# adaLN products of layer 1: from the attention stage to beside the first MLP, in pieces of 256 columns of all four quarters

## The chip, the cores and the metric

The kernel runs on one core of a Trainium2 chip. The metric is the device time of one execution in microseconds (us), lower is better. The program names five engines: PE (TensorE, matrix products), DVE (VectorE), ACT (ScalarE), POOL (GpSimd) and SP (SyncE, which issues the DMA transfers). Each engine runs its own instructions strictly in the order in which they stand; semaphores make one wait for another.

## The reference, cut to what matters

Two layers over 1280 tokens (1024 latent, 256 context) of 1024 channels. Each layer is a mixer and a squared-ReLU MLP, each with a normalised and modulated input and a gated output. The modulation (adaLN) of layer l is

```python
mod = jax.nn.silu(cond) @ ada_w[l] + ada_b[l]      # (1024) @ (1024, 6144), for c and for c_ctx
shift1, scale1, gate1, shift2, scale2, gate2 = split(mod, 6)
h  = rms_norm(x, g1) * (1 + scale1) + shift1
x  = x + gate1 * mixer(h)                          # layer 0: DeltaNet and window attention; layer 1: RG-LRU
h2 = rms_norm(x, g2) * (1 + scale2) + shift2
x  = x + gate2 * (square(relu(h2 @ ff_w1)) @ ff_w2)
```

`cond` has two rows: `c` for the latent tokens, `c_ctx` for the context tokens. `ada_w[l]` is 24 MB. The products of layer 1 are not needed before the end of layer 0's MLP, where layer 1's first norm is applied.

## The kernel before, in words

All is float32 by name. The large products split each factor into a high and a low part of type fp32r and add three products (`gemm_tile`, L463): high by high (L466), low by high (L467) and high by low (L468). Weights come by SP in halves of 256 KB into `wraw` buffers; ACT casts the high part `whi`, POOL or DVE subtracts to get `wlo` (`wload`, L439).

The stages are: input projection of layer 0 (to about 460 us of the span), the attention stage `dn_attention` (460 to 936 us), the output projection (`OutProj`, `hhi`/`hlo` are its input's two parts, made by `split`, L564 and L565), the first MLP (`ff`), the RG-LRU mixer `mix1`, its output projection and the second MLP.

The attention stage goes over five groups of DeltaNet tiles in the order `DN_ORDER`. A group has two halves, called half-steps here. In each half-step `dn_post` prepares two tiles (L1588, L1596, L1604), `dn_step` advances the states (L1635, L1642, L1645; the new state is added on DVE at L1647), and `att_next` lets the window attention go on by one piece (L1791, L1828, L1832; softmax on ACT and DVE, L1818 on POOL or DVE). `finish` and `finish2` complete a tile: a chain of small DVE and POOL operations, transposes on PE (L1681) and a product into `x` at L1684.

Between them `ada_next` advances the adaLN products. `ada` handles a third `q` of the 6144 columns at a time, that is 2048 columns as four quarters `j` of 512. Its 16 pieces of 512 KB each are loaded by L297 into buffers that `whi`/`wlo` use later, and each piece is two products at L300: 32 columns of weights (`sc`, the silu of the conditions) against 512 columns of `adaw`, one for each of two quarters, into 32 partitions each of the PSUM bank `ps_ad`. Five thirds are done in this stage: two of layer 0 and three of layer 1, 80 pieces. At a third's end the sums are copied (L304), transposed (L307, four products) and biased (L310). The list `RATES` says how many pieces are let go after each step.

In the MLP, `ff1` makes one block of 128 hidden channels (24 products for each of three token tiles, of 512, 512 and 256 tokens) into banks `ps_mm`, and `ff2` multiplies two blocks back into 8 output chunks by 3 token tiles, six products for each into banks `ps_w` (L518 to L520), which DVE adds into `x` (L521). The last `ff2` also feeds the next norm: ACT squares each chunk (L396), PE sums it over channels (L332, into a `ps_w` bank held meanwhile), and the sums are spread again (L368, L369, one more bank) for `apply`. PSUM has four `mm` and four `w` banks here.

The order on each engine is made by a scheduler that simulates the program when it is built and takes, of what is ready by its simulation, what has the highest priority; mostly that is the order in the source.

Of the kernel before, what the change touches and what calls it, by code (L numbers as in the profile page):

```python
# [8 lines left out]
F32 = mybir.dt.float32  # L9
F32R = mybir.dt.float32r  # L10
AF = mybir.ActivationFunctionType
# [9 lines left out]
KC = 8  # L21
# [86 lines left out]
def pack(I):  # L108
    f = lambda a: np.ascontiguousarray(np.asarray(a))
    o = {}  # L110
    x = np.concatenate([f(I["x_sample"])[0], f(I["x_prompt"])[0]], axis=0)
    o["xT"] = f(x.T.reshape(KC, 128, T).transpose(1, 0, 2))

    def chunks(w, cols=None):
        w = f(w)
        K, N = w.shape
        return f(w.reshape(K // 128, 128, N // 128, 128).transpose(2, 1, 0, 3).reshape(N // 128, 128, K))

    w_in = f(I["ab_w_in"])[0]
    hp = np.arange(512).reshape(2, 2, 2, 64).transpose(0, 2, 1, 3).reshape(512)  # L120
    qa, ka, va, gate = [w_in[:, 512 * i + hp] for i in range(4)]
    ab = w_in[:, 2048:2080]
    qb = w_in[:, 2080:2592].reshape(D, 2, 4, 64).transpose(0, 2, 1, 3).reshape(D, 512)
    kb, vb = w_in[:, 2592:2720], w_in[:, 2720:2848]
    o["w_in0"] = chunks(np.concatenate([ka, qa, kb, vb, va, qb, gate], axis=1))
    o["w_ab"] = f(ab.reshape(KC, 128, 32).transpose(1, 0, 2).reshape(128, 256))
    wo = f(I["ab_w_out"])[0]
    wob = wo[512:].reshape(2, 4, 64, D).transpose(1, 0, 2, 3).reshape(512, D)
    o["w_out0"] = chunks(np.concatenate([wo[hp], wob], axis=0))
    o["w_in1"] = chunks(f(I["c_w_in"])[0])  # L130
    o["w_out1"] = chunks(f(I["c_w_out"])[0])
    o["ff1"] = np.stack([chunks(f(I["ff_w1"])[l]) for l in range(2)])
    o["ff2"] = f(f(I["ff_w2"]).reshape(2, NFC, 128, D))
    aw = f(I["ada_w"])
    o["ada"] = f(aw.reshape(2, KC, 128, 3, 2048).transpose(0, 3, 1, 2, 4).reshape(6, KC, 128, 2048)[1:])
    o["ada0"] = f(aw[0, :, :2048].reshape(KC, 128, 2, KC, 128).transpose(3, 1, 0, 2, 4).reshape(KC, 128, 2048))
    lw = np.zeros((8, 128, 2, 2, 128), np.float32)
    for gi, nm in enumerate(("lru_w_a", "lru_w_x")):
        w = f(I[nm])[0]
        for d in range(2):  # L140
            for n in range(16):
                lw[n // 2, 64 * (n % 2):64 * (n % 2) + 64, d, gi, 64 * (n % 2):64 * (n % 2) + 64] = w[d, n]
    o["lruw"] = f(lw.reshape(8, 128, 512))
    p = np.zeros((128, NPAR), np.float32)

    def put(n, v):
        a, w = PARAMS[n]
        p[:, a:a + w] = v

    cols = lambda v: f(v).reshape(-1, 128).T  # L150
    for l in range(2):
        put(f"n1g{l}", cols(f(I["norm1_g"])[l]))
        put(f"n2g{l}", cols(f(I["norm2_g"])[l]))
        put(f"adab{l}", cols(f(I["ada_b"])[l]))
    put("cond", np.stack([cols(f(I["c"])[0]), cols(f(I["c_ctx"]))], axis=-1).reshape(128, 16))
    cw, cb = f(I["ab_conv_w"])[0], f(I["ab_conv_b"])[0]
    perm = np.concatenate([512 + hp, hp, 1024 + hp])
    put("abcw", cw[:, perm].reshape(4, 12, 128).transpose(2, 1, 0).reshape(128, 48))
    put("abcb", cols(cb[perm]))
    put("dtb", f(I["dn_dt_bias"])[0].reshape(1, 16))  # L160
    put("alog", f(I["dn_a_log"])[0].reshape(1, 16))
    two = lambda v: np.concatenate([f(v)[0]] * 2)[:, None]
    put("qng", two(I["attn_q_norm_g"]))
    put("kng", two(I["attn_k_norm_g"]))
    put("dng", two(I["dn_norm_g"]))
    put("ccw", f(I["c_conv_w"])[0].reshape(4, 8, 128).transpose(2, 1, 0).reshape(128, 32))
    put("ccb", cols(f(I["c_conv_b"])[0]))
    d8 = lambda v: f(v).reshape(2, 8, 128).transpose(2, 0, 1).reshape(128, 16)
    put("lba", d8(f(I["lru_b_a"])[0]))
    put("lbx", d8(f(I["lru_b_x"])[0]))  # L170
    put("lam", d8(f(I["lru_lambda"])[0]))
    put("h0", d8(f(I["state_lru"])[0, 0]))
    put("sink", f(I["attn_sink"])[0].reshape(1, 8))
    o["par"] = p
    o["con"] = make_consts()
    o["drow"] = make_decay_rows()
    o["rope"] = np.stack(make_rope(), axis=1)
    o["amask"] = make_amask()
    ck = f(I["cache_k"])[0, 0]
    o["ckT"] = f(ck.transpose(1, 2, 0).reshape(128, 256))  # L180
    o["cv"] = f(f(I["cache_v"])[0, 0].reshape(2, 128, 128))
    sd = f(I["state_delta"])[0, 0]
    o["s0"] = f(sd.reshape(2, 4, 2, 64, 64).transpose(2, 3, 0, 1, 4).reshape(128, 512))
    return o
# [105 lines left out]
def ada(g, l, q, alloc, tag="w"):  # L290

    nc = g.nc
    ps = bank(g, tag)
    for k in range(KC):
        for jj in range(2):
            w = alloc()
            nc.sync.dma_start(w.rearrange("p j n -> p (j n)"), g.A["ada"][3 * l + q - 1, k, :, 1024 * jj:1024 * jj + 1024])  # L297
            for i in range(2):
                j = 2 * jj + i
                nc.tensor.matmul(ps[32 * j:32 * j + 32, :], g.sc[:, k, :], w[:, i, :], start=k == 0, stop=k == KC - 1,  # L300
                                 skip_group_check=True)
            yield
    row = wraw(g)
    nc.vector.tensor_copy(row, ps)  # L304
    pt = bank(g, tag)
    for s in range(4):
        nc.tensor.transpose(pt[:, 128 * s:128 * s + 128], row[:, 128 * s:128 * s + 128], g.con["ident"])  # L307
    b = g.par[f"adab{l}"][:, 16 * q:16 * q + 16].rearrange("p (j s) -> p j s", s=4)
    for c in range(2):
        nc.vector.tensor_tensor(  # L310
            g.mod[l][:, 16 * q:16 * q + 16, c].rearrange("p (j s) -> p j s", s=4),
            pt.rearrange("p (s j x) -> p j s x", s=4, j=4)[:, :, :, c], b, op=ALU.add)
    yield


def mod_cols(g, l, which):
# [160 lines left out]
            evac(o, ti, ps[:cols, :tw])  # L477


def ff(g, l, xt, hhi, hlo, Gt, pend, after):  # L480
    nc = g.nc
    pool = g.fp
    hid = {}
    w2 = {}

    def ff1(*cs):
# [3 lines left out]
        for ti, (t0, tw) in enumerate(TT):  # L490
            for c in cs:
                hh, hl = hid[c]
                ps = bank(g, "mm")
                gemm_tile(g, ps[:, :tw], *ws[c], hhi[ti], hlo[ti])
                if pend and c == cs[-1]:
                    pend.pop(0)()
                r = pool.tile([128, 512], F32, tag="ffr", name="ffr", bufs=2)
                nc.scalar.activation(r[:, :tw], ps[:, :tw], AF.Relu)  # L498
                nc.scalar.activation(hh[:, t0:t0 + tw], r[:, :tw], AF.Square)  # L499
                s = pool.tile([128, 512], F32, tag="ffs", name="ffs", bufs=2)  # L500
                nc.vector.tensor_tensor(s[:, :tw], r[:, :tw], r[:, :tw], op=ALU.mult)  # L501
                nc.gpsimd.tensor_tensor(hl[:, t0:t0 + tw], s[:, :tw], hh[:, t0:t0 + tw], op=ALU.subtract)  # L502
# [50 lines left out]
class OutProj:  # L553
# [13 lines left out]
    def finish(self, cut, Gt, after):  # L567

        g, nc, ws = self.g, self.g.nc, self.ws
        xt = []  # L570
# [21 lines left out]
                evac(o, ti, ps)  # L592

        pairs = [(o, ti) for o in range(4) for ti in range(3)]
        run(pairs[:8], KC - 1)
        for p in pairs[8:]:
            run([p])
        ws += [wload(g, self.wsrc[o]) for o in range(4, KC)]
        for ti in range(3):
# [36 lines left out]
    return after, left, h  # L636


def block(g, l, op, cut, after):

    nc = g.nc
    At, Bt, Gt = mod_cols(g, l, 2)
    step, left, h = norm_steps(g, (At, Bt), ff_scratch(g), {1: 4, 2: 4}, {1: 5, 2: 6})
    xt = op.finish(cut, g.mod[l][:, 16:24, :], step)
    ff(g, l, xt, *h["h"], Gt, left, lambda o, ti: after(o, ti, xt[ti]))


def ff_pools(g, es, order):
# [11 lines left out]
def emit(nc, tc, A, stages=None, dbg=None):  # L660
    with ExitStack() as es:
# [2 lines left out]
        g.Dx = g.dp.tile([128, KC, T], F32, name="dx")  # L664
        mix = mix0(g, A["xT"], es)
        g.hp = es.enter_context(tile_pool(g, "hp", side="right"))
        psum_cfg(g, es, mm=4, w=4)
        ab = mod_cols(g, 1, 1)[:2]

        def end1(o, ti, x):  # L670
            if o % 2:
# [2 lines left out]

        with ExitStack() as e2:
            ff_pools(g, e2, ("fp", "wx"))
            step, left, h1 = norm_steps(g, ab, ff_scratch(g), {1: 2, 2: 3}, {1: 5, 2: 7})

            def end0(o, ti, x):
                step(o, ti, x)  # L680
                if o % 4 == 3:
                    t0, tw = TT[ti]
# [3 lines left out]
            for ti in range(3):  # L686
                for k in (0, 2, 4):
                    op.split(ti, k, k + 2)
            block(g, 0, op, 6, end0)
        with ExitStack() as e2:  # L690
            op = mix1(g, h1["h"], left, e2)
        with ExitStack() as e2:
# [836 lines left out]
LATE, OPEN = 0, 0  # L1529
PS = dict(w=3, ad=1, s2=2)  # L1530
NB = dict(XW=3, QI=3, VS=3, kt=3, aP=7)
RATES = [3, 0, 0, 2, 0, 1, 0, 0, 0, 0, 0, 5, 1, 0, 0, 3, 1, 4, 3, 6, 3, 10, 8, 9, 2, 8, 1, 3, 5, 3]
PRI = dict(ada=20, att=-100, step=-1000, post=-200, post0=-200, post1=0, fin=0, late=0)


def dn_attention(g, es, open_mix):
# [198 lines left out]
        na[0] += 1  # L1735
        return g.wp.tile([128, 2, 512], F32, tag=("whi0", "wlo0", "whi1", "wlo1")[na[0] % 4], name="adaw")

    ada_left = (x for l, q in ((0, 1), (0, 2), (1, 0), (1, 1), (1, 2)) for x in ada(g, l, q, aw, "ad" if "ad" in PS else "w"))
    rates = list(RATES)
    for gr in DN_ORDER:  # L1740
        step_group(gr)
# [135 lines left out]
```

## Time and profile before

| | |
|---|---|
| median of three runs | 3308.31 us (3306.94 to 3312.88) |
| the profiled execution, its own time | 3308.6 us |
| its span in the trace | 3306.8 us |
| PE busy | 3150.0 us, 95% |
| DVE, ACT, POOL busy | 1783.5, 1117.5, 714.3 us |
| mean granted clock of PE | 0.976 of full speed |

The span is the time from the first to the last instruction in the trace; the execution's own time is 1.8 us longer. "Busy" is the time in which at least one instruction ran on the engine. Products overlap in PE's pipeline, so what a product costs in a stream is read from start to start, not from its duration.

### The profile page before, as it was taken

What the parts mean: (1) busy time and instruction counts of PE and PEld (TensorE: products, weight loads), DVE (VectorE), ACT (ScalarE), POOL (GpSimd) and SP (SyncE); (2) the same over time, 40 slices, a digit from 0 to 9 for tenths busy, and PEclk for the clock granted to TensorE, in tenths of its full rate; (3) what the DMA queues carried; (4) which work ended last, traced back from release to release, by engine and by line L of the source; (5) the groups of instructions that cost most, each with busy time, mean ns of one, the idle gap of its engine ahead of it and who ended that gap; (6) DMA issues with size and microseconds to landing.
All of it is one profiled execution on the core that took longest, in us unless ns stands there. A gap on an engine that the chain in (4) does not pass through costs nothing.

```text
span 3306.8 us, 50448 instructions
## 1 busy us (share of the span) xinstructions
PE 3150.0 (95%) x20311; PEld 2555.8 (77%) x20311; DVE 1783.5 (54%) x3080; ACT 1117.5 (34%) x2004; POOL 714.3 (22%) x637
## 2 busy tenths in 40 slices
PE   8989966899999999999999999998999999999999
PEld 5867754665568788888888877886778888888888
DVE  5549887667633544444444447778164444444444
ACT  5455523453332321212121236787142121212121
POOL 0000004455432321212121211000142222222220
PEclk9999987999999999999999999999999999999999
DMA  5356777446951011101010121111211111111111
GB/s 201 86 144 171 182 182 207 127 125 212 285 195 33 32 39 32 45 32 45 33 45 32 45 74 41 40 36 43 82 39 45 39 42 36 41 36 40 38 39 70
DMA packets 219272, 273.90 MB, mean 83 GB/s; under 512 B 71578, under 2 KB 125626, under 8 KB 219038
## 3 DMA queue, kind: packets, MB, share of 16 engines
q1 hardware_dynamic: 219038, 270.68, 27.2%
q8 instruction: 159, 2.61, 0.3%
q14 instruction: 75, 0.61, 0.1%
HBM read 223.69 MB, written 46.92 MB: 82 GB/s over the span
## 4 chain that ended last, share of the span: by engine, by line
PE 76%; DVE 8%; DMA 3%; ACT 3%; issue 2%; POOL 1%; SPq 1%; DVEq 0%; ACTq 0%; POOLq 0%
PE ps_mm L466 13%; PE ps_mm L467 13%; PE ps_mm L468 13%; PE ps_w L518 9%; PE ps_w L519 9%; PE ps_w L520 9%; DVE prod L1473 2%; PE ps_ad L300 2%; PE ps_w L1832 1%; PE ps_w L1828 1%; PE ps_w L332 1%; DVE Vinv L1474 1%; DMA adaw<-ada 1%; PE ps_w L1604 1%; PE ps_s L1791 1%
## 5 line engine op out<-in xcount | busy, mean ns | idle before, releaser
L466 PE MATMUL ps_mm<-hhi,whi 128*128 128x512 f32 (+2 forms) x2768 | 991.1, 359 | 21.0 <-ACT hhi L564 13.5
L467 PE MATMUL ps_mm<-hlo,whi 128*128 128x512 f32 (+2 forms) x2768 | 990.1, 358 | 11.0 <-POOL hlo L427 10.8
L468 PE MATMUL ps_mm<-hhi,wlo 128*128 128x512 f32 (+2 forms) x2768 | 987.8, 358 | 0.7 <-POOL wlo L457 0.7
L521 DVE SCALAR_TENSOR_TENSOR x<-ps_w,mod,x 128x512 f32<-128x512 f32 (+1 forms) x768 | 504.1, 660 | 590.9 <-PE ps_w L520 590.9
L466 PEld LDWEIGHTS ps_mm<-hhi,whi 128*128 128x128 f32 (+1 forms) x2768 | 525.8, 190 | 105.2 <-ACT hhi L564 13.9
L467 PEld LDWEIGHTS ps_mm<-hlo,whi 128*128 128x128 f32 (+1 forms) x2768 | 526.0, 190 | 92.9 <-POOL hlo L427 14.3
L468 PEld LDWEIGHTS ps_mm<-hhi,wlo 128*128 128x128 f32 (+1 forms) x2768 | 526.2, 190 | 79.8 <-issue 6.4
L519 PE MATMUL ps_w<-hidl,whi 128*128 128x512 f32 (+1 forms) x1536 | 546.5, 356 | 1.7 <-POOL hidl L502 1.7
L518 PE MATMUL ps_w<-hidh,whi 128*128 128x512 f32 (+1 forms) x1536 | 545.8, 355 | 0.0
L520 PE MATMUL ps_w<-hidh,wlo 128*128 128x512 f32 (+1 forms) x1536 | 543.8, 354 | 0.0
L502 POOL TENSOR_TENSOR hidl<-ffs,hidh 128x512 fp32r<-128x512 f32 (+1 forms) x192 | 226.5, 1180 | 1217.4 <-ACT hidh L499 977.8
L498 ACT ACTIVATE ffr<-ps_mm 128x512 f32<-128x512 f32 (+1 forms) x192 | 100.4, 523 | 902.7 <-PE ps_mm L468 883.6
L453 ACT CAST whi<-wraw 128x512 fp32r<-128x512 f32 x365 | 211.8, 617 | 516.4 <-PE ps_w L519 301.0
L501 DVE TENSOR_TENSOR ffs<-ffr 128x512 f32<-128x512 f32 (+1 forms) x192 | 164.3, 855 | 331.6 <-ACT ffr L498 327.9
L518 PEld LDWEIGHTS ps_w<-hidh,whi 128*128 128x128 f32 x1536 | 290.5, 189 | 45.7 <-issue 1.4
L519 PEld LDWEIGHTS ps_w<-hidl,whi 128*128 128x128 f32 x1536 | 290.4, 189 | 45.0 <-POOL hidl L502 2.5
L520 PEld LDWEIGHTS ps_w<-hidh,wlo 128*128 128x128 f32 x1536 | 289.7, 189 | 41.9 <-issue 0.6
L457 POOL TENSOR_TENSOR wlo<-wraw,whi 128x512 fp32r<-128x512 f32 (+1 forms) x157 | 210.4, 1361 | 259.7 <-ACT whi L453 157.7
L457 DVE TENSOR_TENSOR wlo<-wraw,whi 128x512 fp32r<-128x512 f32 x208 | 147.8, 733 | 90.9 <-ACT whi L453 90.8
L499 ACT ACTIVATE hidh<-ffr 128x512 fp32r<-128x512 f32 (+1 forms) x192 | 107.4, 560 | 5.8
L580 DVE SCALAR_TENSOR_TENSOR x<-ps_mm,mod,x 128x512 f32<-128x512 f32 (+1 forms) x40 | 25.9, 655 | 149.0 <-PE ps_mm L468 138.5
L300 PE MATMUL ps_ad<-adaw,sc 128*32 128x512 f32 x320 | 81.7, 653 | 18.8 <-DMA adaw<-ada 18.8
(377 smaller groups left out, 3272.4 us busy)
## 6 DMA issues: line engine op xcount, KB each, us to landing
wraw<-ff SPq DMA_DIRECT2D x256, 256.0 KB
adaw<-ada SPq DMA_DIRECT2D x80, 512.0 KB
wraw<-w_in SPq DMA_DIRECT2D x76, 256.0 KB
dn<-NI SPq DMA_DIRECT2D x40, 256.0 KB
aw<-ada SPq DMA_DIRECT2D x16, 512.0 KB
wraw<-w_out SPq DMA_DIRECT2D x32, 256.0 KB
dkv<-tok SPq DMA_DIRECT2D x20, 256.0 KB
rtab<-rope SPq DMA_DIRECT2D x10, 512.0 KB
```

What stands on the lines that cost most here:

```text
L300: nc.tensor.matmul(ps[32 * j:32 * j + 32, :], g.sc[:, k, :], w[:, i, :], start=k == 0, stop=k == KC - 1, skip_group_check=True)
L453: nc.scalar.copy(hv[:, o:o + half], raw[:, :half])
L457: e.tensor_tensor(lv[:, o:o + half], raw[:, :half], hv[:, o:o + half], op=ALU.subtract)
L466: nc.tensor.matmul(ps, whi[:, k, :], hhi[:, k, :], start=first and k == k0, stop=False)
L467: nc.tensor.matmul(ps, whi[:, k, :], hlo[:, k, :], start=False, stop=False)
L468: nc.tensor.matmul(ps, wlo[:, k, :], hhi[:, k, :], start=False, stop=last and k == k1 - 1)
L501: nc.vector.tensor_tensor(s[:, :tw], r[:, :tw], r[:, :tw], op=ALU.mult)
L502: nc.gpsimd.tensor_tensor(hl[:, t0:t0 + tw], s[:, :tw], hh[:, t0:t0 + tw], op=ALU.subtract)
L518: nc.tensor.matmul(ps[:, :tw], whi[:, o, :], hh[:, t0:t0 + tw], start=f == 0, stop=False)
L519: nc.tensor.matmul(ps[:, :tw], whi[:, o, :], hl[:, t0:t0 + tw], start=False, stop=False)
L520: nc.tensor.matmul(ps[:, :tw], wlo[:, o, :], hh[:, t0:t0 + tw], start=False, stop=f == 1)
L521: nc.vector.scalar_tensor_tensor(xt[ti][:, o, :], ps[:, :tw], Gt[:, o, cc:cc + 1], xt[ti][:, o, :], op0=ALU.mult, op1=ALU.add)
```

## The change

The three thirds of layer 1 leave the attention stage. A new generator `ada_late` does them, and it is advanced from `ff1` of the first MLP: once after the block's product over the first token tile and once after the second, where no step of the norm is due. What is left is drained when the first output chunk of the last `ff2` is complete (`end0`), where the modulation columns of layer 1 are now also made. A piece is still 512 KB, but holds 256 columns of all four quarters instead of 512 columns of two: its products are four of 32 by 256, in four groups of 32 partitions of the bank. All pieces use one buffer `adw`, and the copy at a third's end uses it too. The weights are repacked on the host as `ada1`. `ada_late` takes a PSUM bank of its own, so from the first output projection to the program's end there are three `w` banks instead of four, and `OutProj` starts seven products early instead of eight. `RATES` is thinned in the late steps.

```diff
-    ada_left = (x for l, q in ((0, 1), (0, 2), (1, 0), (1, 1), (1, 2)) for x in ada(g, l, q, aw, "ad" if "ad" in PS else "w"))
+    ada_left = (x for q in (1, 2) for x in ada(g, 0, q, aw, "ad" if "ad" in PS else "w"))
-RATES = [3, 0, 0, 2, 0, 1, 0, 0, 0, 0, 0, 5, 1, 0, 0, 3, 1, 4, 3, 6, 3, 10, 8, 9, 2, 8, 1, 3, 5, 3]
+RATES = [3, 0, 0, 2, 0, 1, 0, 0, 0, 0, 0, 3, 1, 0, 0, 2, 1, 2, 1, 2, 1, 2, 2, 2, 1, 2, 1, 2, 2, 1]

+def ada_late(g):
+    nc = g.nc
+    sc = g.fp.tile([128, 64], F32, name="scl")
+    nc.gpsimd.memset(sc, 0.0)
+    nc.scalar.activation(sc[:, 0:16], g.par["cond"], AF.Silu)
+    for q in range(3):
+        ps = bank(g, "ad")
+        for k in range(KC):
+            for p in range(2):
+                w = g.fp.tile([128, 4, 256], F32, tag="adw", name="adw", bufs=1)
+                nc.sync.dma_start(w.rearrange("p j n -> p (j n)"), g.A["ada1"][q, k, :, 1024 * p:1024 * p + 1024])
+                yield
+                for j in range(4):
+                    nc.tensor.matmul(ps[32 * j:32 * j + 32, 256 * p:256 * p + 256], sc[:, 2 * k:2 * k + 32], w[:, j], start=k + p == 0,
+                                     stop=k == KC - 1, skip_group_check=True)
+        yield
+        row = g.fp.tile([128, 4, 256], F32, tag="adw", name="adr", bufs=1).rearrange("p j n -> p (j n)")[:, :512]
+        ada_end(g, 1, q, ps, bank(g, "w"), row)

 (in ff1, after a block's product over token tile ti)
                 if pend and c == cs[-1]:
                     pend.pop(0)()
+                elif c == cs[-1] and ti < 2:
+                    next(side, None)

-        psum_cfg(g, es, mm=4, w=4)
-        ab = mod_cols(g, 1, 1)[:2]
+        psum_cfg(g, es, mm=4, w=3, ad=1)
+        ab = []
+            side = ada_late(g)
             def end0(o, ti, x):
+                if not ab:
+                    list(side)
+                    ab.extend(mod_cols(g, 1, 1)[:2])
                 step(o, ti, x)

-        run(pairs[:8], KC - 1)
-        for p in pairs[8:]:
+        run(pairs[:7], KC - 1)
+        for p in pairs[7:]:
```

`ada_end` is the old end of `ada` (copy, transposes, bias) as a function. Lines of the changed kernel stand up to 34 higher.

On PE, the end of the attention stage before, from a product of the last steps to the first of the output projection (L300 and L307 are adaLN, L1681 the transposes of `finish2`, L466 the output projection):

```order
L1635 MATMUL ps_w<-VS,XW 64x64 x8
L300 MATMUL ps_ad<-adaw,sc 32x512 x2
L1828 MATMUL ps_w<-con,aP 128x128 x4
L300 MATMUL ps_ad<-adaw,sc 32x512 x2
L1642 MATMUL ps_w<-VS,kt 64x64 x8
...
L300 MATMUL ps_ad<-adaw,sc 32x512 x2
L1681 MATMUL ps_w<-con,oB 128x2x64 x4
L300 MATMUL ps_ad<-adaw,sc 32x512 x6
L1681 MATMUL ps_w<-con,oB 128x2x64 x4
L300 MATMUL ps_ad<-adaw,sc 32x512 x6
L307 MATMUL ps_ad<-con,wraw 128x128 x4
L466 MATMUL ps_w<-hhi_10204,whi 128x512
```

The same place on PE in the changed kernel (L1676 and L1679 are the old L1642 and L1645, L1862 and L1866 the old L1828 and L1832, L1715 the old L1681, L493 the old L466):

```order
L313 MATMUL ps_ad<-con,wraw 128x128 x4
L1862 MATMUL ps_w<-con,aP 128x128
L1676 MATMUL ps_w<-VS,kt 64x64 x8
L1679 MATMUL ps_w<-VS,QI 64x64 x8
L1866 MATMUL ps_w<-wraw,Vtok 64x256 x2
L1862 MATMUL ps_w<-con,aP 128x128 x4
L1866 MATMUL ps_w<-wraw,Vtok 64x256 x2
L1715 MATMUL ps_w<-con,oB 128x2x64 x8
L493 MATMUL ps_mm<-hhi_9978,whi 128x512
```

No adaLN piece stands between the last steps any more; only the transposes of layer 0's last third do.

On PE in the first MLP of the changed kernel, one piece in the middle of it (L336 is `ada_late`, L548 to L550 `ff2`, L493 to L495 `ff1`):

```order
L495 MATMUL ps_mm<-hhi_10697,wlo 128x512
L336 MATMUL ps_ad<-adw,scl 32x256 x3
L548 MATMUL ps_w<-hidh,whi 128x512
L549 MATMUL ps_w<-hidl,whi 128x512
...
L549 MATMUL ps_w<-hidl,whi 128x256
L550 MATMUL ps_w<-hidh,wlo 128x256
L336 MATMUL ps_ad<-adw,scl 32x256
L493 MATMUL ps_mm<-hhi_10698,whi 128x512
```

The four products of this piece stand apart: three, then twelve products of `ff2`, then the fourth. Of the 48 pieces 15 are torn in this way; the other 33 stand as four in a row.

On SP, the loads at the start of the first MLP in the changed kernel (L333 loads a piece, L478 a half of weights, for the output projection or the MLP):

```order
L478 DMA wraw<-w_out 128x512 x3
L478 DMA wraw<-ff 128x512 x12
L333 DMA adw<-ada 128x1024 x7
L478 DMA wraw<-ff 128x512 x4
L333 DMA adw<-ada 128x1024 x6
L478 DMA wraw<-ff 128x512 x26
```

Seven and six loads of pieces stand in a row, and since there is one buffer, each waits for the products of the piece before it; the weights behind them wait too.

## Rows read from the trace of the kernel before

**Rows 1.** The page: busy time and share of the span, instructions.
```profile
PE 3150.0 (95%) x20311; PEld 2555.8 (77%) x20311; DVE 1783.5 (54%) x3080; ACT 1117.5 (34%) x2004; POOL 714.3 (22%) x637
```

**Rows 2.** Busy us by stretch: PE, PEld, DVE, ACT, POOL, clock, DMA share, GB/s.
```profile
598.00:743.00 145.00, 131.12 (x2016) 97.92 (x2016) 98.56 (x204) 79.66 (x185) 78.57 (x64) 0.96 0.40 120
743.00:795.00 52.00, 47.47 (x574) 27.85 (x576) 34.39 (x71) 17.43 (x40) 22.05 (x18) 0.97 0.82 255
795.00:837.00 42.00, 38.15 (x553) 24.96 (x548) 31.43 (x77) 17.59 (x43) 23.50 (x19) 1.00 0.62 199
837.00:879.00 42.00, 42.00 (x534) 22.72 (x534) 30.02 (x76) 15.53 (x42) 21.87 (x19) 1.00 1.02 277
879.00:922.00 43.00, 42.58 (x576) 22.99 (x574) 30.20 (x82) 15.46 (x43) 18.39 (x17) 1.00 0.85 264
1250.00:1300.00 50.00, 50.00 (x264) 43.10 (x263) 21.15 (x31) 10.57 (x20) 12.28 (x10) 1.00 0.14 43
1950.00:1975.00 25.00, 21.75 (x142) 15.87 (x135) 16.45 (x29) 13.02 (x24) 7.21 (x5) 0.93 0.27 100
```

**Rows 3.** The same stretches, PE and PEld of line L300 alone.
```profile
743.00:795.00 52.00, 14.55 (x64) 2.15 (x64) 0.97 0.82 255
795.00:837.00 42.00, 6.13 (x32) 0.99 (x32) 1.00 0.62 199
837.00:879.00 42.00, 16.06 (x62) 2.34 (x64) 1.00 1.02 277
879.00:922.00 43.00, 16.65 (x70) 2.26 (x68) 1.00 0.85 264
```

**Rows 4.** PE timeline, attention: start us, us, what, count.
```profile
864.07 1.05 PE L300 MATMUL ps_ad<-adaw,sc 128*32 128x512 f32 x4
865.05 1.15 PE L1635 MATMUL ps_w<-VS,XW 128*64 128x64 f32 x32
```

**Rows 5.** PE timeline, layer 0's first products at the kernel's start.
```profile
54.04 0.28 PE L466 MATMUL ps_mm<-hhi,whi 128*128 128x256 f32 x1
54.16 0.28 PE L466 MATMUL ps_w<-hhi,whi 128*128 128x256 f32 x1
54.37 0.64 PE L1075 MATMUL ps_w<-aw,sc 128*32 128x256 f32 x8
54.94 0.38 PE L467 MATMUL ps_mm<-hlo,whi 128*128 128x256 f32 x1
55.16 0.28 PE L468 MATMUL ps_mm<-hhi,wlo 128*128 128x256 f32 x1
...
62.66 0.50 PE L466 MATMUL ps_mm<-hhi,whi 128*128 128x512 f32 x1
62.99 0.39 PE L466 MATMUL ps_gg<-hhi,whi 128*128 128x512 f32 x1
63.22 0.28 PE L466 MATMUL ps_mm<-hhi,whi 128*128 128x256 f32 x1
```

**Rows 6.** DVE timeline at the end of the attention stage.
```profile
922.36 0.41 DVE L1654 TENSOR_TENSOR oB<-oB,ps_w 128x256 f32<-128x256 f32 x1
...
925.16 0.75 DVE L1684 SCALAR_TENSOR_TENSOR x<-ps_w,par,gt 128x512 f32<-128x512 f32 x1 [1.66 <-PE ps_w L1681]
...
931.62 0.75 DVE L1684 SCALAR_TENSOR_TENSOR x<-ps_w,par,gt 128x512 f32<-128x512 f32 x1 [0.81 <-PE ps_w L1681]
933.52 1.23 DVE L565 TENSOR_TENSOR hlo<-x,hhi 128x1024 fp32r<-128x1024 f32 x1 [1.16 <-ACT hhi L564]
...
935.26 3.49 DVE L565 TENSOR_TENSOR hlo<-x,hhi 128x1024 fp32r<-128x1024 f32 x3
```

**Rows 7.** PE timeline at the same place.
```profile
935.40 0.66 PE L307 MATMUL ps_ad<-con,wraw 128*128 128x128 f32 x4 [0.84 <-DVE wraw L304]
936.38 0.49 PE L466 MATMUL ps_w<-hhi,whi 128*128 128x512 f32 x1 [0.32 <-ACT hhi L564]
938.81 0.80 PE L467 MATMUL ps_w<-hlo,whi 128*128 128x512 f32 x1 [1.93 <-DVE hlo L565]
```

**Rows 8.** SP and ACT timeline, first MLP: a load of weights and its first use.
```profile
1210.04 1.52 SPq L451 DMA_DIRECT2D wraw<-ff  x2
1212.75 0.62 ACT L453 CAST whi<-wraw 128x512 fp32r<-128x512 f32 x1 [1.49 <-DMA wraw<-ff]
```

**Rows 9.** The page: the accumulation of the MLP on DVE, busy us and mean ns.
```profile
L521 DVE SCALAR_TENSOR_TENSOR x<-ps_w,mod,x 128x512 f32<-128x512 f32 (+1 forms) x768 | 504.1, 660 | 590.9 <-PE ps_w L520 590.9
```

More of the change, by code (lines that the diff above doesn't have):

```diff
@@ L134, in pack @@
     aw = f(I["ada_w"])
-    o["ada"] = f(aw.reshape(2, KC, 128, 3, 2048).transpose(0, 3, 1, 2, 4).reshape(6, KC, 128, 2048)[1:])
+    o["ada"] = f(aw[0].reshape(KC, 128, 3, 2048).transpose(2, 0, 1, 3)[1:])
+    o["ada1"] = f(aw[1].reshape(KC, 128, 3, 4, 2, 256).transpose(2, 0, 1, 4, 3, 5).reshape(3, KC, 128, 2048))
     o["ada0"] = f(aw[0, :, :2048].reshape(KC, 128, 2, KC, 128).transpose(3, 1, 0, 2, 4).reshape(KC, 128, 2048))
@@ L296, in ada @@
             w = alloc()
-            nc.sync.dma_start(w.rearrange("p j n -> p (j n)"), g.A["ada"][3 * l + q - 1, k, :, 1024 * jj:1024 * jj + 1024])
+            nc.sync.dma_start(w.rearrange("p j n -> p (j n)"), g.A["ada"][q - 1, k, :, 1024 * jj:1024 * jj + 1024])
             for i in range(2):
@@ L302, in ada, with ada_end @@
             yield
-    row = wraw(g)
+    ada_end(g, l, q, ps, bank(g, tag), wraw(g))
+    yield
+def ada_end(g, l, q, ps, pt, row):
+    nc = g.nc
     nc.vector.tensor_copy(row, ps)
-    pt = bank(g, tag)
     for s in range(4):
@@ L312, in ada @@
             pt.rearrange("p (s j x) -> p j s x", s=4, j=4)[:, :, :, c], b, op=ALU.add)
-    yield
+def ada_late(g):
+    nc = g.nc
+    sc = g.fp.tile([128, 64], F32, name="scl")
[11 more added lines that the diff above has]
+                                     stop=k == KC - 1, skip_group_check=True)
+        yield
+        row = g.fp.tile([128, 4, 256], F32, tag="adw", name="adr", bufs=1).rearrange("p j n -> p (j n)")[:, :512]
+        ada_end(g, 1, q, ps, bank(g, "w"), row)
 def mod_cols(g, l, which):
@@ L477, in gemm, with ff @@
             evac(o, ti, ps[:cols, :tw])
-def ff(g, l, xt, hhi, hlo, Gt, pend, after):
+def ff(g, l, xt, hhi, hlo, Gt, pend, after, side):
     nc = g.nc
@@ L636, in norm_steps, with block @@
     return after, left, h
-def block(g, l, op, cut, after):
+def block(g, l, op, cut, after, side=()):
     nc = g.nc
@@ L644, in block @@
     xt = op.finish(cut, g.mod[l][:, 16:24, :], step)
-    ff(g, l, xt, *h["h"], Gt, left, lambda o, ti: after(o, ti, xt[ti]))
+    ff(g, l, xt, *h["h"], Gt, left, lambda o, ti: after(o, ti, xt[ti]), iter(side))
 def ff_pools(g, es, order):
@@ L688, in emit @@
                     op.split(ti, k, k + 2)
-            block(g, 0, op, 6, end0)
+            block(g, 0, op, 6, end0, side)
         with ExitStack() as e2:
```

## The prediction

> **What bounds the kernel now.** Read the page's busy times first: PE is busy for 95% of the span, no other engine for more than 54% [rows 1]. So work on PE counts wherever PE waits for nothing, and the question at each place is whether it does. The table of busy time by stretch answers that. In the first MLP PE is busy 50.00 of 50 us [rows 2]: whatever is added there is added to the time. In the attention stage two kinds of stretch differ. From 598 to 743 us stand four half-steps without any adaLN product: 145 us, PE busy 131.1, so 36.3 us for a half-step, 32.8 of them PE and 3.5 its waits [rows 2]. From 743 to 922 us stand the last four, 179 us, and with them adaLN: 64, 32, 62 and 70 records of L300, four to a piece, so 57 pieces [rows 3]. There PE is nearly full (170.2 of 179 us), and DMA too (up to 277 GB/s) [rows 2]. So adaLN is what makes these half-steps long. The two questions are how short they get without it, and what the same products cost in a stage that has no gap.
>
> **What leaves the attention stage.** Of 80 pieces 48 go. The first 16 stand before 743 us in both orders, and 16 of the 57 in the last half-steps stay, so 41 leave these and 7 leave the tail behind 922 us. From the start of a piece to the next product 0.98 us pass [rows 4], so 41 pieces are 40 us of PE. The half-steps don't get shorter by all of that. Without L300, PE's busy time in them is 47.5 − 14.6 = 32.9, then 32.0, 25.9 and 25.9 us [rows 2, 3]; the last two are lighter. With the 3.5 us of waits that a half-step without filler has, the first two come to 36.4 and 35.5. In the last two DVE has 30.0 and 30.2 us of work [rows 2], so I put them at 32 each, not at 29.4. Sum 136 us; the 16 pieces that stay add 15.7 and fill the 3.5 us of waits of the half-step that holds most of them, so 148 against 179: **31 us saved**. The bounds: four half-steps as long as those before 743 (145) and 16 pieces with nothing hidden, at 1.1 each, 163, saves 16; no waits at all (116.7 + 15.7 = 132) saves 47.
>
> The tail, from the last state (922.36) to the output projection's second product (938.81, the first that is followed by others) [rows 6, 7]: DVE stood 1.66 us for L1681, which stood behind pieces; and the first L467 waited for the fourth `hlo` (935.26 + 3.49), where the new order begins with a product that needs only the first (933.52 + 1.23 = 934.75): 4.0. Together with the copy of the sums between them that is **6 us saved** (0 to 8: the chain of `finish` itself stays, and PE has nothing to do in it now). The loads of `w_out` no longer stand behind pieces in SP's queue; they bound nothing here, so I count nothing.
>
> **What comes into the first MLP.** The new form of a piece, four products of 32 by 256, stands in the trace already: layer 0's first third is done that way at the kernel's start. Two passes each make eight records; they take from 54.37 to 54.94, 0.57 us, against 0.98 for the old form. But in that stream there is more. Products of 256 columns follow each other at 0.12 us (54.04 to 54.16); the one before the group takes 0.21 and the one behind it 0.22. Behind another group the first product of 512 columns takes 0.33 where the next takes 0.23 [rows 5]. So each entry costs 0.1 us and each exit 0.1, and a piece costs 0.57 + 0.19 = 0.76 us. The Trainium skill, "TensorEngine Tiling (Array Packing)", Key Properties, says that changing the tiling mode drains TensorE; that rule speaks against this change, the rows agree with it, and without such drains the sum below would be lower by 63 × 0.19 = 12 us.
>
> The order tears 15 of the 48 pieces into three and one. Three take as long as four; the fourth alone has its own entry and exit (0.19) and its two passes, which is at most 0.57 and which I put at 0.46: 0.65. So 48 × 0.76 + 15 × 0.65 = 36.5 + 9.8 = 46.3. The transposes of three thirds move along: four products take 0.66 [rows 7], with entry and exit 0.85, so 2.6. Together **48.9 us added** to a stage where PE has no gap (27 if entries, exits and lone fourths cost nothing; 51 if a lone fourth costs 0.57 too).
>
> **Loads.** Each piece's load waits for the products of the piece before it. A half of weights (256 KB) takes 2.7 us from issue to use [rows 8]; 512 KB at the 277 GB/s of [rows 2] take 0.95 more, so an estimate of 3.7, with the semaphores about 4 us. In the order nearly all pieces stand over 6 us of products apart. At the MLP's start eight stand closer: four at about 4.2 us (17 or 18 products of 0.23 or their like), three at 2.6 to 3.3, one at 0.9, where PE waits for the norm anyway. **2 us** (0 to 4). Weights behind a piece's load in SP's queue are issued at the latest when the piece before has been used; by the order the products that need them then stand 20 us or more behind, and a weight needs some 5 us, so nothing.
>
> **Three `w` banks instead of four.** In the last `ff2` of the first MLP one bank holds a norm's sums and for part of the time a second or the spread rows; three leave one or two for `ff2`, and with one a group of six products can't start before DVE has added the last (0.66 us [rows 9] and two semaphores, about 0.9), of which the sums on PE cover half. Eight or ten groups at 0.4 are 4 us. But PE has waits there now (21.75 busy of 25 [rows 2]), so some of it is hidden. In the rest of the two MLPs a group takes 1.4 us and DVE 0.66, so two banks in hand are enough unless DVE is late by over 2 us. **4 us** (0 to 12, where the mixer of layer 1 and both MLPs lose a little too).
>
> DVE, POOL and ACT get a few small instructions in the MLP, where they are busy for under half of the time [rows 2]: nothing.
>
> Sum on the profiled execution: 3308.6 − 31 − 6 + 48.9 + 2 + 4 = **3326.5 us**. The median of the runs is 0.3 lower, so I predict **3326 us**, 18 more than before.
>
> **The rivals.**
>
> (A, faster) *PE stays the bound of the last half-steps, and what leaves it is all gain.* For it: PE is busy 170 of 179 us there, and its waits are under 4 us in a half-step even without filler. Then 47 us go there and 8 in the tail, 55, and with 46 to 50 added (torn pieces partly standing where PE waits) and nothing lost to banks the time is 3300 to 3304; with a lone fourth or entries cheaper than read, 3295. It decides from the point where the half-steps with 25.9 us of PE work really take under 30. Against it: DVE has 30 us of work in each.
>
> (B, no change) *The half-steps shorten by 36 and the torn fourths cost little*, because they stand at a boundary where PE changes its mode or waits anyway: 3308.6 − 36 − 6 + 39 + 2 + 2 = 3310.
>
> (C, much slower) *The loads do bound*: a piece's load waits for PE, the weights behind it wait on SP, and with three banks PE waits for DVE in many of the 32 blocks of each MLP. At 0.5 us for each of 64 blocks that is 32 us on top of a saving of 31: near 3350. For it: seven loads in a row in SP's queue. Against it: the distances above.
>
> That the change doesn't do what it says is excluded by the order: no piece of layer 1 is left in the attention stage.
>
> **How the numbers follow.** The forecast's own range, 3315 to 3340, has a chance of 0.55. A has 0.20, B 0.17, C 0.08. A measurement of this kernel tells about 0.2%, 6.6 us, from no change: 3301.7 to 3314.9. Faster is A, 0.20; within is B and a little of the forecast's edge, 0.19; slower is the rest, 0.61. The range that should hold the time 8 times in 10 reaches into A and up to the lower part of C: 3297 to 3342.
>
> **What would show it.** In the changed trace: the four last half-steps together at 148 us (132 would be A); the output projection's first products some 37 us earlier than 936 us; a piece in the first MLP with 0.57 us to the next product, 0.33 for the first product of 512 columns behind it, and lone fourths of about 0.46; from the output projection's start to the end of the first MLP some 52 us more than before, PE still without waits in its middle; a wait of PE for `adw` only in its first 100 us, a few us in all; the mixer of layer 1 and the second MLP as long as before within 4 us. I am wrong if the attention stage loses over 45 us, or if the products of the pieces take less than 0.6 us of PE's time each in the stream, or if PE waits for weights.

## The result: 3365.14 us, 56 us slower than before

The changed kernel takes 3365.14 us (median of 4 runs, 3363.93 to 3370.94), the kernel before 3308.67 us (median of 4 runs, one more than before the prediction). The ratio is 1.0171 (95% interval 1.0158 to 1.0183). I had predicted 3326 us with a range up to 3342: the direction was right, and the loss is three times as large.

PE has a little more work, and waits more. The page's first line, after:

```profile
PE 3172.5 (94%) x20503; PEld 2562.8 (76%) x20503; DVE 1831.1 (54%) x3080; ACT 1112.0 (33%) x2007; POOL 737.5 (22%) x638
```

PE is busy for 22.5 us more than before [rows 1], but the span is 56.8 us longer, so most of the loss is PE's waiting. Where that is, marks show that stand in both traces: the state (DVE) from which [rows 2] count the last four half-steps, the last state, the output projection's second product, and the first and last `ff2` product of each MLP (PE). In us:

| from mark to mark | before | after | difference | predicted |
|---|---|---|---|---|
| start to the last four half-steps | 743.1 | 750.0 | +6.9 | 0 |
| last four half-steps | 179.0 | 150.7 | -28.3 | -31 |
| tail, to the output projection | 16.8 | 14.0 | -2.8 | -6 |
| output projection and first MLP | 1048.5 | 1099.1 | +50.6 | +51 to +55 |
| mixer of layer 1, its output projection | 451.7 | 477.4 | +25.7 | 0 to +4 |
| second MLP | 864.3 | 868.9 | +4.6 | 0 |

The last four half-steps after, in the columns of [rows 2]:

```profile
750.00:787.00 37.00, 32.60 (x512) 24.28 (x512) 31.51 (x70) 17.67 (x40) 24.46 (x20) 1.00 0.48 139
787.00:833.50 46.50, 45.15 (x577) 26.16 (x577) 31.11 (x73) 17.61 (x42) 22.78 (x18) 1.00 0.74 236
833.50:870.00 36.50, 31.02 (x489) 22.69 (x488) 30.02 (x74) 16.15 (x44) 22.79 (x20) 0.91 0.40 125
870.00:901.00 31.00, 26.01 (x479) 20.29 (x480) 27.25 (x79) 14.52 (x39) 15.18 (x16) 0.89 0.18 55
```

The second holds the 16 pieces that stayed, and PE is full there; in the other three PE waits, and DVE's 27 to 32 us are near the length. In the last two the granted clock is 0.91 and 0.89, where [rows 2] have 1.00 and PE had almost no gap. A piece in the first MLP, and then a torn one (PE: start us, us):

```profile
1288.63 0.39 PE L495 MATMUL ps_mm<-hhi,wlo 128*128 128x512 f32 x1
1288.95 0.64 PE L336 MATMUL ps_ad<-adw,scl 128*32 128x256 f32 x8
1289.52 0.50 PE L548 MATMUL ps_w<-hidh,whi 128*128 128x512 f32 x1
1289.86 0.39 PE L549 MATMUL ps_w<-hidl,whi 128*128 128x512 f32 x1
...
1337.33 0.63 PE L336 MATMUL ps_ad<-adw,scl 128*32 128x256 f32 x6
1337.89 0.50 PE L548 MATMUL ps_w<-hidh,whi 128*128 128x512 f32 x1
...
1340.18 0.62 PE L336 MATMUL ps_ad<-adw,scl 128*32 128x256 f32 x2
1340.73 0.50 PE L493 MATMUL ps_mm<-hhi,whi 128*128 128x512 f32 x1
```

Whole pieces take 0.57 us, threes 0.56 and a lone fourth 0.55; the product ahead takes 0.32 and the one behind 0.34, where the next has 0.23: the sizes of [rows 5] once more.

What I had not seen coming stands in the mixer. PE's longest waits there and in the first products behind it (us in total, times, the longest), and the wait of a gate, before and then after:

```profile
PE ps_mm L466 <- ACT hhi L564: 13.5, 2, 13.0
...
PE ps_w L813 <- ACT rr L757: 0.7, 1, 0.7
```
```profile
PE ps_w L847 <- ACT rr L791: 14.8, 6, 10.6
PE ps_mm L493 <- ACT hhi L594: 13.3, 2, 12.6
```

The first line of after was 0.7 us before and is 14.8 now. L847 is the first of three products of a gate of the RG-LRU; L791 is ACT, which applies the sigmoid to a gate's bank `ps_w` and so frees it. The longest of these waits, on PE and on ACT, after:

```profile
2315.73 0.47 PE L847 MATMUL ps_w<-xh,lwhi 128*128 128x512 f32 x1 [1.69 <-DVE lwhi L825]
...
2317.98 0.96 PE L849 MATMUL ps_w<-xh,lwlo 128*128 128x512 f32 x3 [0.62 <-DVE lwlo L826]
2329.55 0.80 PE L847 MATMUL ps_w<-xh,lwhi 128*128 128x512 f32 x1 [10.61 <-ACT rr L791]
2330.14 0.63 PE L848 MATMUL ps_w<-xl,lwhi 128*128 128x512 f32 x1
2330.57 0.63 PE L849 MATMUL ps_w<-xh,lwlo 128*128 128x512 f32 x1
```
```profile
2315.86 2.62 ACT L791 ACTIVATE aa<-rr,m 128x1280 f32<-128x1280 f32 x2
2318.38 2.60 ACT L791 ACTIVATE rr<-rr,p 128x1280 f32<-128x1280 f32 x2
2321.00 1.28 ACT L791 ACT_TABLE_LOAD   x1
2322.30 2.43 ACT L791 ACTIVATE rr<-rr 128x1280 f32<-128x1280 f32 x2
2324.74 1.28 ACT L791 ACT_TABLE_LOAD   x1
2326.04 1.46 ACT L791 ACTIVATE x<-x 128x512 f32<-128x512 f32 x3
2327.51 1.28 ACT L791 ACT_TABLE_LOAD   x1
2328.81 0.69 ACT L791 ACTIVATE rr<-ps_w,par 128x512 f32<-128x512 f32 x1
```

The gates come in fours, two directions by two gates for a token tile. With three banks PE has done three at 2318.9 and stands before the fourth. The bank is freed by a sigmoid that stands on ACT behind a whole chain of other functions, most of them the previous column's (`act` keeps their order by a dependency): 13 us of them, three table loads of 1.28 us each included. Before, the same place on PE:

```profile
2261.81 0.39 PE L813 MATMUL ps_w<-xh,lwhi 128*128 128x512 f32 x1
...
2263.64 1.08 PE L815 MATMUL ps_w<-xh,lwlo 128*128 128x512 f32 x4
2264.55 0.39 PE L466 MATMUL ps_mm<-hhi,whi 128*128 128x512 f32 x1
...
2278.38 0.50 PE L813 MATMUL ps_w<-xh,lwhi 128*128 128x512 f32 x1 [0.66 <-ACT rr L757]
```

There all four fit, and products of the last projection (L466 to L468) fill most of the time in which ACT runs the same chain: PE waits 0.66 us. After, no product of that projection is left in PE's order here: behind the third gate stand 27 gate products in a row (L847 to L849), and the projection's products have run before. With another number of banks the scheduler makes another order, so what a bank costs is always the wait and the order together.

The clock is lower behind the wait too. Busy times and granted clock, in the columns of [rows 2], behind the wait and 6 us later:

```profile
2329.50:2335.50 6.00, 5.95 (x14) 4.70 (x15) 6.00 (x12) 3.64 (x6) 0.00 (x0) 0.50 0.01 3
2336.00:2342.00 6.00, 5.93 (x33) 4.94 (x32) 4.13 (x5) 5.91 (x10) 0.00 (x0) 1.00 0.00 0
```

Behind the 10.61 us in which PE stood idle the granted clock is 0.50, the lower of its two levels (1.2 and 2.4 GHz), and products follow each other at 0.43 us (2330.14 to 2330.57) instead of 0.23; in the second stretch it is 1.00 again. Twelve or thirteen products at the slower pace are an estimate of 2.5 us.

### The profile page after: what moved, and what is told of

Read it like the earlier page. It is cut to its first block, busy times and chain, and to the rows that moved or that the text cites. A ratio compares the mean times of both kernels' runs of the same rounds, so it can differ in the third digit from the quotient of the medians.

```text
span 3363.6 us, 50829 instructions
## 1 busy us (share of the span) xinstructions
PE 3172.5 (94%) x20503; PEld 2562.8 (76%) x20503; DVE 1831.1 (54%) x3080; ACT 1112.0 (33%) x2007; POOL 737.5 (22%) x638
## 4 chain that ended last, share of the span: by engine, by line
PE 72%; DVE 11%; ACT 4%; DMA 3%; issue 2%; POOL 1%; SPq 1%; DVEq 0%; ACTq 0%; POOLq 0%
PE ps_mm L493 13%; PE ps_mm L494 13%; PE ps_mm L495 12%; PE ps_w L548 9%; PE ps_w L549 9%; PE ps_w L550 9%; DVE prod L1507 2%; PE ps_ad L336 1%; ACT rr L791 1%; PE ps_w L1866 1%; DVE Vinv L1508 1%; PE ps_w L359 1%; DVE NI L1474 1%; DVE rr L872 1%; PE ps_w L1862 1%
## 5 line engine op out<-in xcount | busy, mean ns | idle before, releaser
L493 PE MATMUL ps_mm<-hhi,whi 128*128 128x512 f32 (+2 forms) x2784 | 1001.8, 361 | 21.8 <-ACT hhi L594 15.2
L495 PE MATMUL ps_mm<-hhi,wlo 128*128 128x512 f32 (+2 forms) x2784 | 995.7, 359 | 0.0
L551 DVE SCALAR_TENSOR_TENSOR x<-ps_w,mod,x 128x512 f32<-128x512 f32 (+1 forms) x768 | 495.8, 660 | 823.5 <-PE ps_w L550 822.9
L493 PEld LDWEIGHTS ps_mm<-hhi,whi 128*128 128x128 f32 (+1 forms) x2784 | 529.1, 190 | 119.0 <-issue 16.8
L495 PEld LDWEIGHTS ps_mm<-hhi,wlo 128*128 128x128 f32 (+1 forms) x2784 | 529.5, 190 | 83.0 <-issue 8.7
L548 PE MATMUL ps_w<-hidh,whi 128*128 128x512 f32 (+1 forms) x1536 | 549.8, 358 | 6.3 <-ACT whi L480 4.9
L550 PE MATMUL ps_w<-hidh,wlo 128*128 128x512 f32 (+1 forms) x1536 | 538.1, 355 | 0.0
L532 POOL TENSOR_TENSOR hidl<-ffs,hidh 128x512 fp32r<-128x512 f32 (+1 forms) x192 | 244.3, 1285 | 582.4 <-ACT hidh L529 473.6
L548 PEld LDWEIGHTS ps_w<-hidh,whi 128*128 128x128 f32 x1536 | 290.5, 189 | 64.5 <-issue 7.1
L550 PEld LDWEIGHTS ps_w<-hidh,wlo 128*128 128x128 f32 x1536 | 288.9, 189 | 42.5 <-issue 0.4
L531 DVE TENSOR_TENSOR ffs<-ffr 128x512 f32<-128x512 f32 (+1 forms) x192 | 189.6, 1001 | 169.1 <-ACT ffr L528 128.1
L484 DVE TENSOR_TENSOR wlo<-wraw,whi 128x512 fp32r<-128x512 f32 x208 | 178.1, 883 | 22.0 <-ACT whi L480 21.3
```

The lines of the kernel that those rows point to most:

```text
L484: e.tensor_tensor(lv[:, o:o + half], raw[:, :half], hv[:, o:o + half], op=ALU.subtract)
L493: nc.tensor.matmul(ps, whi[:, k, :], hhi[:, k, :], start=first and k == k0, stop=False)
L495: nc.tensor.matmul(ps, wlo[:, k, :], hhi[:, k, :], start=False, stop=last and k == k1 - 1)
L548: nc.tensor.matmul(ps[:, :tw], whi[:, o, :], hh[:, t0:t0 + tw], start=f == 0, stop=False)
L550: nc.tensor.matmul(ps[:, :tw], wlo[:, o, :], hh[:, t0:t0 + tw], start=False, stop=f == 1)
L551: nc.vector.scalar_tensor_tensor(xt[ti][:, o, :], ps[:, :tw], Gt[:, o, cc:cc + 1], xt[ti][:, o, :], op0=ALU.mult, op1=ALU.add)
```

## The experiments

Theory: my terms hold, and the missing 30 us are the missing `w` bank, in the mixer. The rivals: the other order or the late modulation costs the time behind the first MLP; or the pieces cost more than their products.

**The bank handed back.** Once layer 1's sums are done (`end0`, behind `list(side)`, sets `g.four`), the changed kernel's fourth bank joins the rotation of `w`, and the second output projection starts eight products early:

```diff
 def bank(g, tag="w"):
+    if tag == "w" and getattr(g, "four", 0):
+        g.four += 1
+        tag = "ad" if g.four % 4 == 0 else "w"
```

> The changed kernel, with the bank of the adaLN sums handed back as a fourth w bank once layer 1's sums are done (from the first finished chunk of the first MLP's last ff2 on), and eight early products in the second output projection. Theory 'banks': the 25.6 us lost between the end of the first MLP and the start of the second, and the 4.7 us lost in the second MLP, come from three w banks in the mixer; both go, PE's wait for ACT's sigmoid in the mixer (14.8 us) falls under 2 us, and the time is 3335 to 3342 us. Rival 'order': the loss comes from the late modulation and another order, the banks are not what PE waits for: 3360 to 3367 us.

Measured 3333.22 us, ratio to before 1.0053 (1.0040 to 1.0067): a little under the range of "banks". From the end of the first MLP to the second takes 450.1 us instead of 477.4, the second MLP 866.2 instead of 868.9, and the wait of a gate for ACT (L852 here) is back to what it was before:

```profile
PE ps_w L852 <- ACT rr L796: 0.7, 1, 0.7
```

"Order" falls.

**Three banks in the kernel before**, with nothing else changed (`w=3`, `run(pairs[:7])`).

> The kernel before with three w banks instead of four from the first output projection on, and seven early products instead of eight; adaLN stays in the attention stage. Theory 'banks': the loss of the changed kernel behind the first MLP appears here alone: 3308.7 plus 22 to 34, 3331 to 3343 us, nearly all of it between the end of the first MLP and the start of the second. Rival 'order': 3309 to 3314 us.

Measured 3350.40 us, ratio 1.0112 (1.0099 to 1.0126): 37 us, over my bound. The two profiled spans differ by 42.0 us: 26.5 of them stand between the MLPs, 5.8 in the second MLP and 2.9 in the output projection and first MLP. The wait is the same one, to the tenth:

```profile
PE ps_w L813 <- ACT rr L757: 14.8, 6, 10.6
PE ps_mm L466 <- ACT hhi L564: 13.2, 2, 12.6
```

The other 7 us stand ahead of the output projection, up to which all five engines run the instructions of before in the same order: its second product comes at 945.7 instead of 938.8 us. So one execution differs from another by that much there. The +6.9 us of my table is of this kind: its first mark stands at 743.1, 748.4 and 745.3 us in the runs with the order of before, and at 750.0, 747.6, 746.3 and 743.7 in those with the order of after. With the other runs of each order, the second product comes at 938.8, 945.7 and 944.9 us with adaLN in the attention stage, and at 914.6, 914.7, 912.8 and 913.5 without: 29 us apart on average, where I had 37.

**A gate in an `mm` bank.** As the last run, but the fourth gate of each four takes another kind of bank:

```diff
-                    ps = bank(g, "w")
+                    ps = bank(g, "mm" if d and gi else "w")
```

> The kernel before with three w banks, as in the run that takes one away, but the fourth of the mixer's four gate groups of each token tile takes an mm bank. Theory 'gates': the mixer loses 20 us with three banks because its gate groups come in fours and ACT frees the banks only when its own chain of functions reaches them: the mixer comes back to 344 us (from 363.7), and the rest of the loss stays (6.8 us in the second output projection, 5.8 in the second MLP): 3350 less 17 to 20. Rival: any bank missing from the rotation costs the same, the mm banks now bind, and the time stays at 3345 us or more.

Measured 3321.92 us, ratio 1.0026 (1.0016 to 1.0036): 28 us less than with three banks, more than I expected (the ratios differ by as much). From the first MLP's end to the first sums of the next norm it takes 339.5 us (343.9 before, 363.7 with three banks). The wait of L813 for ACT is gone, and of the one for `hhi` half is left, a gain that the kernel before does not have either:

```profile
PE ps_mm L466 <- ACT hhi L564: 6.9, 1, 6.9
```

The second MLP keeps its loss (869.0). So the bank is missed at the gates: that is shown. That all 28 us are the gates' is not: 6.3 of them are the wait for `hhi`, and why that one halves is open.

**No pieces**, the price of what was added (the edit is shortened).

```diff
-        for k in range(KC):
-            for p in range(2):
...
+        nc.vector.memset(ps, 0.0)
+        for _ in range(16): yield
```

> The changed kernel with the loads and the products of layer 1's adaLN pieces left out (the sums are set to zero; copy, transposes and bias stay). By the trace of the changed kernel a piece takes 0.57 us to the next product and the lone fourths 0.55 us, with the products beside them 46 us: 3365 less 44 to 48, 3317 to 3321 us, with the first MLP shorter by that and nothing else changed. Rival: PE's waits, hidden by the pieces now, come back, and under 35 us are saved: 3330 us or more.

Measured 3318.06 us, inside the range, and 47 less than the changed kernel (53 by the ratios, 1.0012 and 1.0171). The output projection and first MLP take 1050.0 instead of 1099.1 us: 49.1 us for 48 pieces with their loads, 1.02 us each; the other rows of the table stay within 4 us. I had 46.3 and 2 for these.

**More torn pieces**, a dose of one term: `tc.cur_priority` is lowered by 400 for the four products (with the fourth bank handed back).

> The changed kernel with the fourth bank handed back, and with the pieces' products given another priority, by which 13 pieces are torn into four single products, 3 into three and one, and 32 stay whole: 90 separate groups instead of 63, 55 single products instead of 15. Theory 'modes': each single product costs its two passes (0.55 us) and each group an entry and an exit (0.2 us): 40 singles more at 0.55, 12 threes fewer and 1 whole piece fewer at 0.57, 27 groups more at 0.2: 22.0 - 7.4 + 5.4 = 20 us more than the run with the fourth bank, all in the first MLP. Rival: only the products count (0.14 us each, four to a piece), and nothing changes.

Measured 3351.27 us, against 3333.22 for the kernel it is made from (20 us by the ratios, 1.0113 and 1.0053); output projection and first MLP 1117.1 instead of 1097.6: 19.5 us, where I expected 20. What tears a piece costs the two passes and a change of mode each time, whatever it holds.

**The cheaper form left in the attention stage.** The kernel before, each piece as four products of 32 by 256 (shortened; `p` is the half of the 512 columns):

```diff
-            for i in range(2):
-                nc.tensor.matmul(ps[32 * j:32 * j + 32, :], g.sc[:, k, :], w[:, i, :], ...)       # j = 2 * jj + i
+            for j in range(4):
+                nc.tensor.matmul(ps[32 * j:32 * j + 32, 256 * p:256 * p + 256], g.sc[:, k, :], w[:, 256 * j:256 * j + 256], ...)
```

> The kernel before with adaLN left in the attention stage, its 80 pieces in the changed kernel's form (four products of 32 by 256, one for each quarter, instead of two of 32 by 512; weights repacked on the host). Theory 'PE': the last half-steps are bound by PE, where a piece then costs 0.57 to 0.76 us instead of 0.98: 57 pieces save 12 to 23 us, 3286 to 3297 us. Rival 'DMA': the loads (up to 277 GB/s) bound those half-steps, and nothing is gained: 3304 to 3311 us.

Measured 3308.18 us, ratio 0.9984 (0.9973 to 0.9995): hardly anything. PE's busy time in the last four half-steps falls from 170.2 [rows 2] to 158.5 us, but they take 179.7 us as before. What was products became waits for loads; from 743 to 939 us:

```profile
PE ps_ad L300 <- DMA adaw<-ada: 15.0, 14, 2.4
```

Before, the same wait:

```profile
PE ps_ad L300 <- DMA adaw<-ada: 3.8, 5, 1.6
```

"PE" falls: PE's work is 11.7 us less and its wait for loads 11.2 us more, so there the loads are the next bound, at once behind PE.

**The pieces spread out**, in the cheap form and in the old one.

```diff
-RATES = [3, 0, 0, 2, 0, 1, 0, 0, 0, 0, 0, 5, 1, 0, 0, 3, 1, 4, 3, 6, 3, 10, 8, 9, 2, 8, 1, 3, 5, 3]
+RATES = [3, 0, 0, 2, 0, 1, 3, 2, 3, 3, 3, 3, 3, 3, 3, 3, 3, 3, 3, 3, 4, 4, 3, 4, 4, 3, 4, 3, 3, 3]
```

> The kernel before with the pieces in the four-quarter form, as in the run with the quarters in the attention stage, and the 80 pieces spread evenly over the half-steps from the third on, instead of most of them in the last five. There PE's waits for the pieces' loads had grown from 3.8 to 15.0 us. Theory 'loads': the last half-steps are bound by the loads (248 GB/s from 743 to 939 us), spread out the loads hide, and the cheaper form shows: 3280 to 3296 us. Rival 'chain': the half-steps are bound by their own chain of steps and any piece lengthens them, wherever it stands: 3302 to 3312 us.

> The kernel before, pieces in their old form (two products of 32 by 512), with the same even spread over the half-steps. It tells the spread from the form. Theory 'loads': loads hide, but a piece takes 0.98 us of PE, and only some 3.5 us of a half-step are free: 3298 to 3308 us, slower than the four-quarter form with the same spread by 10 to 20 us. Rival 'chain': 3302 to 3312 us, as the four-quarter form.

Cheap form: 3296.18 us, ratio 0.9947 (0.9932 to 0.9962), 0.2 us above the range. Old form: 3305.94 us, ratio 0.9979 (0.9967 to 0.9991), inside its range, and 9.8 us slower than the cheap form. So each alone is worth 0.2%, and both together 0.5% here and 0.4% when run again below: that the form gains more once the loads have room is not clear of the noise by the times. In the cheap form PE's waits for loads in the last half-steps are back to before's:

```profile
PE ps_ad L300 <- DMA adaw<-ada: 3.8, 9, 0.6
```

**Earlier still**: `RATES` lets 12, 12, 11, 10, 9, 9, 9 and 6 pieces go in the third to the tenth half-step (10 in the sixth, one fewer than the expectation says).

> As the run with the four-quarter form spread evenly, with the pieces let go still earlier (11 or 12 in each of the third to sixth half-steps, 6 in the last). Theory 'loads': in the third to fifth half-step PE has waits and the loads room (0.40 to 0.83 of the DMA engines' time), in the seventh to ninth not; a few us more are saved, 3290 to 3295 us. Rival 'chain': by the even spread the waits are used up; what goes at the end comes back in the middle, 3295 to 3300 us.

Both theories missed. Measured 3312.35 us, ratio 0.9991 (0.9979 to 1.0004). The output projection's second product comes at 944.6 us instead of 933.1, and from 562 to 939 us PE waits 12.3 us for loads, against 6.2 with the even spread. Why PE waits longer for loads that start earlier was not tried; it stays open.

**The best of both**, with the even spread run once more beside it.

> The run with the four-quarter form spread evenly (four w banks), and the fourth of the mixer's gate groups in an mm bank, as in the run that did this with three w banks, where the mixer took 339.5 us against 343.9 in the kernel before. Theory 'gates': five banks for the gates let PE run further ahead of ACT; the mixer takes 4 us less, 3290 to 3294 us. Rival: with four w banks nothing waits for a gate bank any more, and the time stays at 3294 to 3298 us.

> The run with the four-quarter form spread evenly once more, on this chip, beside the next version: 3294 to 3300 us, 0.4 to 0.6% under the kernel before.

Even spread again 3300.18 us, ratio 0.9962 (0.9949 to 0.9975); with the gate in an `mm` bank 3302.71 us, ratio 0.9968 (0.9955 to 0.9982). These are the same: with four `w` banks the gates don't need a fifth. The even spread of the cheap form is the fastest of the versions tried, by about 0.4 to 0.5% against before.

## Why the prediction was wrong

**Attention stage, -31 and -6.** Right in kind, too large by 8 us. The half-steps without pieces don't shrink to PE's work, as rival A has it, but to 31 to 37 us: 150.7 us against 148 in this trace, 153.8 on average over the four runs of this order. The third of them was to take 32 us and takes 36.5: PE is busy for 31.0 us there, not 25.9, with nearly the same products, at a granted clock of 0.91. I had taken PE's work from a stretch at 1.00 and did not ask whether that would hold. The tail takes 14.0 us against 10.8; there PE waits for the chain of `finish` at the end: on DVE, after, the last state and the last product's addition into `x`:

```profile
900.66 0.42 DVE L1681 TENSOR_TENSOR S<-St,ps_w 128x256 f32<-128x256 f32 x1
...
911.44 0.75 DVE L1718 SCALAR_TENSOR_TENSOR x<-ps_w,par,gt 128x512 f32<-128x512 f32 x1 [1.23 <-PE ps_w L1715]
```

The row that I took for the last state before (922.36, L1654) is the output's sum; the state stands at 922.0, which changes nothing. Over all runs of either order the stage is 29 us shorter, not 37.

**Pieces, +48.9, and their loads, +2.** Right. 49.1 us for products and loads by experiment; the transposes, which I had at 2.6, stay in that run and were not priced alone; the waits for `adw` in the first MLP come to 1.7 us. One size was off: a lone fourth takes 0.55 us, not 0.46, which is 15 times 0.09 or 1.4 us. The Trainium skill, "TensorE: Matmul & The Clock Gate", section "Why this matters for your kernels", says that products for distinct column groups run concurrently. The rows agree: one product, three or four take 0.55, 0.56 and 0.57 us.

**Three `w` banks, +4 (0 to 12).** This step failed. I priced it from the norm at the end of the first MLP and from `ff2`, where a bank is freed by one DVE operation of 0.66 us [rows 9], and left the mixer at "a little". There the term held: the output projection and first MLP lose 1.5 us without pieces (1050.0 against 1048.5) and 2.9 with the bank taken alone, and PE's waits for DVE to empty a `ps_w` bank come to 1.0 us in all. But a bank is held not for as long as the operation that empties it, but until its engine gets there, and in the mixer this is ACT, whose order is fixed, behind 13 us of other functions. The gates come in fours, and four banks held them. Of my own signs, that the mixer be as long as before within 4 us is the one that failed: 25.7 us, and 4.6 in the second MLP. The term is 32 us (3365.14 to 3333.22, after; 39 by the ratios to before) or 37 (before), most of it behind the first MLP. With 32 in place of 4, and 29 in place of 37, the sum on the profiled execution is 3326.5 + 28 + 8 = 3362.5, against 3365.4 measured. The 32 comes from the changed kernel's own time, so this tests the rest of the sum and not the 32.

The Trainium skill, "Perfetto Trace Analysis", section "Optimizing Tensor Performance", asks that independent groups of products rotate through different banks, so that emptying one overlaps the next. The traces agree, and show the price where a stage is one bank short: 10.6 us before the fourth gate.

Rival C named the time (near 3350) and "three banks", but in the wrong place: PE was to wait for DVE in the blocks of the MLPs. That loads hold the first MLP up, its other half, is wrong. Of the 32 us, the wait for ACT (14.8 us) and the clock behind it (2.5 us, an estimate) are read from rows. One output tile less started early in the second output projection (21 products of 0.23 us, an estimate of 4.8 us) and the second MLP's 3 to 6 us are put down to the same bank only because most of them goes when it is given back, and they stay when only the gates get one; waits of their own hardly show. Some 5 to 7 us of the 32 are not accounted for.

## What to carry to other kernels

When a change takes a PSUM bank, list every stage that rotates through that tag until the program's end, and for each ask how many groups stand in a row and when the engine that empties them gets there, not how long the emptying takes. Work moved out of a stage with gaps into one without costs its full price: 48 pieces cost 49 us beside the MLP. In the attention stage, spread out, all 80 in the cheap form reach the output projection at 932 us, against 914 with only 32 pieces there (three runs against four): 18 us, though those 32 had the old form, so part of the difference is the form. And a cheaper form can be eaten up by the next bound behind it: in the last half-steps PE's work fell by 11.7 us, its waits for loads rose by 11.2, and the time fell by 0.2%.

## What was unexpected of the hardware

The same instructions in the same order reached the output projection at 938.8, 945.7 and 944.9 us in three executions; whether they ran on the same chip is not known for the first, and the other two ran on different ones. A mark of a single trace within 7 us in that part proves nothing; the intervals of the timed runs do.
